# A fused residual add and layer norm on one Trainium2 core: turns of 8 rows instead of 4 on ScalarE and VectorE, and last stores of 8 and 8 rows instead of 12 and 4

## The chip, the cores and the metric

The kernel runs on one core of one Trainium2 chip. The metric is device time in microseconds (us) of one execution. Before the change it is 238.29 us (median of 3 runs, 238.26 to 238.30).

A "row" below is a set of 128 rows of the input, one for each partition: [128, 512] fp32, 256 KB. There are 128 such rows, numbered 0 to 127.

## The reference

```python
# x, residual: [16, 1024, 512] fp32; gamma = 1, beta = 0 in this draw; eps = 1e-5
def reference(x, residual, gamma, beta, eps):
    z = x + residual
    mean = np.mean(z, axis=-1, keepdims=True)
    var = np.var(z, axis=-1, keepdims=True)
    z_norm = (z - mean) / np.sqrt(var + eps)
    return (gamma * z_norm + beta).astype(np.float32)
```

x and residual are read (67 MB), the result is written (34 MB).

## The kernel before

SyncE (SP) issues all bulk transfers into one DMA queue, in the order of a written plan. `x48+16` loads rows 48 to 63 of x, `r` loads residual, `o` stores. The buffer of z holds 64 rows, that of residual 32, so a load of x waits for an old store to land, and a load of residual waits for POOL's adds.

```python
PLAN = """
x0+8 r0+8 x8+8 r8+8 x16+16 r16+16 x32+16 r32+16
x48+16 r48+16 o0+16 r64+16 x64+16 o16+16 r80+16 x80+16
o32+16 r96+16 x96+8 x104+8 o48+16 r112+16 x112+8 x120+8
o64+16 o80+16 o96+16 o112+12 o124+4
"""
ADDS = [4, 4, 8] * 7 + [4] * 4     # rows of one POOL add
TURN = 4                           # rows of one turn
SETS = 2                           # turns in one loop body
LAP = SETS * TURN
```

POOL adds residual into z. ScalarE takes a turn of rows: it makes their means (one pass for each row), then their sums of squares (a second pass), then one square-root for the whole turn. VectorE follows with two passes of its own and a reciprocal.

```python
    with act.Fori(0, total // LAP) as lap:            # ScalarE, a loop on the chip
        ...
        for j in range(SETS):                         # unrolled in the body
            due = act.snap(r0 + (j + 1) * TURN)
            act.wait_ge(s_dve, due)
            act.wait_ge(s_add, due)
            for k in range(TURN):
                i = act.activation(out=junk_m[k][:, :], in_=zk[k], func=ACT.Identity,
                                   scale=-inv_d, accum_out=nm[j][:, k : k + 1])
            i.then_inc(s_mean, TURN)
            act.wait_ge(s_mean, due)
            for k in range(TURN):
                i = act.activation(out=junk_s[k][:, :], in_=zk[k], func=ACT.Square,
                                   bias=nm[j][:, k : k + 1], accum_out=ssq[j][:, k : k + 1])
            i.then_inc(s_ssq, TURN)
            act.wait_ge(s_ssq, due)
            act.activation(out=std[j][:, :], in_=ssq[j][:, :], func=ACT.Sqrt, ...).then_inc(s_std, TURN)
    ...
    with dve.Fori(0, total // LAP) as lap:            # VectorE
        ...
        for j in range(SETS):
            dve.wait_ge(s_ssq, due)
            for k in range(TURN):                     # first pass: (z - mean) * gamma
                dve.scalar_tensor_tensor(out=zk[k], in0=zk[k], scalar=nm[j][:, k : k + 1], ...)
            dve.wait_ge(s_std, due)
            dve.reciprocal(out=rstd[j][:, :], in_=std[j][:, :]).then_inc(s_dve, TURN)
            dve.wait_ge(s_dve, due + LAP)
            for k in range(TURN):                     # second pass: * rstd + beta
                i = dve.scalar_tensor_tensor(out=zk[k], ..., scalar=rstd[j][:, k : k + 1], ...)
            i.then_inc(s_out, TURN)                   # stores wait for this
```

## Time and profile before

| | before |
|---|---|
| time | 238.29 us |
| span in the profile | 236.9 us |
| share of the span in which the bulk queue moves data | 99.2% |
| ScalarE, VectorE, POOL busy | 185.5, 177.2, 143.0 us |
| last add lot of POOL starts / last store issued | 192.86 (four adds) / 226.67 us |

From the profile page of the kernel before. Part 1 is busy time by engine; part 3 is the DMA queues with packets, MB and the share of 16 engines' span; part 5 gives, for each group of instructions, the count, busy us and mean ns, and then the idle time ahead of them and what ended it.

```profile
PE 3.7 (2%) x4; PEld 1.2 (0%) x4; DVE 177.2 (75%) x290; ACT 185.5 (78%) x545; POOL 143.0 (60%) x29
...
q1 hardware_dynamic: 4176, 100.67, 99.2%
q14 instruction: 1, 0.01, 0.0%
...
L202 ACT ACTIVATE junk_m<-zbuf 128x512 f32 x128 | 74.9, 585 | 29.1 <-POOL zbuf L180 27.5
L212 ACT ACTIVATE junk_s<-zbuf,nm 128x512 f32 x128 | 88.8, 694 | 1.0
...
L221 ACT ACTIVATE std<-ssq,eps_t 128x4 f32<-128x4 f32 x32 | 9.5, 297 | 3.0
L249 DVE RECIPROCAL rstd<-std 128x4 f32<-128x4 f32 x32 | 5.5, 170 | 0.0
```

No engine is near 100%; the queue q1 is. Queue q14, whose kind the page gives as instruction, has one packet in the whole span.

The table of windows of the kernel before: the stretch in us, then busy us of each engine, the granted clock, the DMA share and GB/s.

```profile
77.00:80.00 3.00, 0.00 (x0) 0.00 (x0) 2.71 (x5) 2.89 (x11) 1.80 (x1) 1.00 1.16 448
190.00:230.00 40.00, 0.00 (x0) 0.00 (x0) 30.39 (x49) 26.16 (x77) 17.96 (x4) 1.00 1.00 432
230.00:231.00 1.00, 0.00 (x0) 0.00 (x0) 0.00 (x0) 0.00 (x0) 0.00 (x0) 1.00 1.03 442
231.00:232.00 1.00, 0.00 (x0) 0.00 (x0) 0.00 (x0) 0.00 (x0) 0.00 (x0) 1.00 0.97 418
232.00:233.00 1.00, 0.00 (x0) 0.00 (x0) 0.00 (x0) 0.00 (x0) 0.00 (x0) 1.00 0.85 360
233.00:236.00 3.00, 0.00 (x0) 0.00 (x0) 0.00 (x0) 0.00 (x0) 0.00 (x0) 1.00 0.71 300
236.00:237.00 1.00, 0.00 (x0) 0.00 (x0) 0.00 (x0) 0.00 (x0) 0.00 (x0) 1.00 0.02 8
```

The queue runs at 432 GB/s from 190 to 230 us; the rate falls as the last store drains (360 GB/s at 232 to 233 us, 300 from there to 236).

The end of the kernel before in the timeline (start us, duration, engine, line, operation; SPq is SyncE issuing a transfer).

```profile
178.18 0.80 SPq L146 DMA_DIRECT2D zbuf<-in_x_dram  x2
...
192.86 17.96 POOL L180 TENSOR_TENSOR zbuf<-zbuf,rbuf 128x2048 f32<-128x2048 f32 x4 [11.62 <-DMA zbuf<-in_x_dram]
...
221.03 0.30 ACT L221 ACTIVATE std<-ssq,eps_t 128x4 f32<-128x4 f32 x1
...
223.92 2.72 DVE L252 SCALAR_TENSOR_TENSOR zbuf<-zbuf,rstd,beta_p 128x512 f32 x4
226.67 0.33 SPq L146 DMA_DIRECT2D out_dram<-zbuf  x1
```

SyncE issues the last loads of x at 178.18 us, because a store has landed. POOL starts its last four adds at 192.86, because the load of rows 112 to 119 has landed. VectorE's last four rows take from 223.92 to 226.64, and the last store (4 rows) is issued at once, while older stores still fill the queue for some six microseconds.

### The profile page before, as it was taken

Reading aid. Unit: us, or ns where it says so; the run is one execution under the profiler, and the core shown is the slowest. Engines: PE = TensorE matmul, PEld = TensorE weight load, DVE = VectorE, ACT = ScalarE, POOL = GpSimd, SP = SyncE. Lnnn points to the kernel's source line nnn. Section 1 sums busy time; section 2 is a strip of 40 time slices with the busy share of each in tenths; the row PEclk is TensorE's granted clock in tenths of the full one; section 3 lists DMA queues with packets and bytes.
Section 4 is the critical chain, followed back from the end, with each engine's and each line's share of the span. In section 5 each row is a group of like instructions: output and inputs, shape, how many; then the busy total and the mean of one; then the engine's idle time right before and its main releaser. Section 6 shows DMA issues by size and latency. Waiting matters only on the chain.

```text
span 236.9 us, 1471 instructions
## 1 busy us (share of the span) xinstructions
PE 3.7 (2%) x4; PEld 1.2 (0%) x4; DVE 177.2 (75%) x290; ACT 185.5 (78%) x545; POOL 143.0 (60%) x29
## 2 busy tenths in 40 slices
PE   0600000000000000000000000000000000000000
PEld 0100000000000000000000000000000000000000
DVE  0001977939699999999898989896989895698920
ACT  2019879497999999999999998979998956999300
POOL 0098920999799699604995059944995049950000
DMA  8999999999999999999999999999999999999996
GB/s 310 443 432 426 426 443 443 443 443 443 426 415 398 443 443 443 426 420 409 431 437 443 443 443 432 420 407 429 443 437 437 409 432 448 437 420 437 426 430 285
DMA packets 4181, 100.68 MB, mean 425 GB/s; under 512 B 466, under 2 KB 466, under 8 KB 468
## 3 DMA queue, kind: packets, MB, share of 16 engines
q1 hardware_dynamic: 4176, 100.67, 99.2%
q14 instruction: 1, 0.01, 0.0%
q10 hardware_dynamic: 4, 0.00, 0.0%
HBM read 67.11 MB, written 33.55 MB: 425 GB/s over the span
## 4 chain that ended last, share of the span: by engine, by line
DMA 71%; POOL 9%; ACT 9%; DVE 2%; issue 2%; SPq 1%; ACTq 0%; DVEq 0%; POOLq 0%
DMA out_dram<-zbuf 49%; DMA rbuf<-in_residual_dram 16%; POOL zbuf L180 9%; DMA zbuf<-in_x_dram 6%; ACT junk_s L212 5%; ACT junk_m L202 4%; SPq L146 1%; DVE zbuf L240 1%; DVE zbuf L252 1%; ACTq L202 0%; DVEq L240 0%; ACT std L221 0%; DVE rstd L249 0%; ACTq L193 0%; POOLq L177 0%
## 5 line engine op out<-in xcount | busy, mean ns | idle before, releaser
L180 POOL TENSOR_TENSOR zbuf<-zbuf,rbuf 128x2048 f32<-128x2048 f32 (+1 forms) x25 | 142.8, 5740 | 67.6 <-DMA zbuf<-in_x_dram 40.8
L240 DVE SCALAR_TENSOR_TENSOR zbuf<-zbuf,nm,gamma_p 128x512 f32 x128 | 87.1, 743 | 46.3 <-ACT junk_s L212 46.3
L202 ACT ACTIVATE junk_m<-zbuf 128x512 f32 x128 | 74.9, 585 | 29.1 <-POOL zbuf L180 27.5
L212 ACT ACTIVATE junk_s<-zbuf,nm 128x512 f32 x128 | 88.8, 694 | 1.0
L252 DVE SCALAR_TENSOR_TENSOR zbuf<-zbuf,rstd,beta_p 128x512 f32 x128 | 87.1, 743 | 1.1
L212 ACT ACTIVATION_READ_ACCUMULATOR junk_s<-zbuf,nm 128x1 f32 x128 | 23.9, 187 | 0.0
L202 ACT ACTIVATION_READ_ACCUMULATOR junk_m<-zbuf 128x1 f32 x128 | 23.9, 187 | 0.0
L221 ACT ACTIVATE std<-ssq,eps_t 128x4 f32<-128x4 f32 x32 | 9.5, 297 | 3.0
L249 DVE RECIPROCAL rstd<-std 128x4 f32<-128x4 f32 x32 | 5.5, 170 | 0.0
L190 ACT ACT_TABLE_LOAD x1 | 1.3, 1283 | 2.7 <-PEq L60 2.7
L132 PE MATMUL gamma_p<-gb_row,ones 1*128 1x512 f32 x2 | 2.0, 1119 | 7.2 <-DMA gb_row<-in_gamma_dram 7.2
L132 PE MATMUL beta_p<-gb_row,ones 1*128 1x512 f32 x2 | 1.9, 1052 | 0.0
L127 DVE MEMSET ones<- 1x128 f32 x1 | 0.2, 165 | 2.0 <-PEq L60 2.0
L132 PEld LDWEIGHTS beta_p<-gb_row,ones 1*128 1x128 f32 x2 | 0.7, 328 | 1.0 <-issue 0.5
L132 PEld LDWEIGHTS gamma_p<-gb_row,ones 1*128 1x128 f32 x2 | 0.5, 308 | 7.1 <-issue 7.1
L288 POOL MEMSET const-float32-0.0<- 128x1 f32 x1 | 0.1, 98 | 0.2 <-issue 0.2
L288 POOL MEMSET const-bfloat16-1.0<- 128x1 bf16 x1 | 0.1, 101 | 0.0
L288 POOL MEMSET const-uint8-127<- 128x1 uint8 x1 | 0.1, 101 | 0.0
L288 POOL MEMSET const-float32-1.0<- 128x1 f32 x1 | 0.1, 98 | 0.0
L128 DVE MEMSET eps_t<- 128x1 f32 x1 | 0.1, 59 | 0.0
## 6 DMA issues: line engine op xcount, KB each, us to landing
rbuf<-in_residual_dram SPq DMA_DIRECT2D x7, 4096.0 KB, 30.5
out_dram<-zbuf SPq DMA_DIRECT2D x7, 4096.0 KB, 28.6
zbuf<-in_x_dram SPq DMA_DIRECT2D x5, 4096.0 KB, 28.9
zbuf<-in_x_dram SPq DMA_DIRECT2D x6, 2048.0 KB, 14.9
rbuf<-in_residual_dram SPq DMA_DIRECT2D x2, 2048.0 KB, 15.7
out_dram<-zbuf SPq DMA_DIRECT2D x1, 3072.0 KB, 13.5
out_dram<-zbuf SPq DMA_DIRECT2D x1, 1024.0 KB, 10.2
gb_row<-in_gamma_dram ACTq DMA_DIRECT2D x1, 2.0 KB
```

The source lines that it names most:

```text
L127: nc.vector.memset(ones[:, :], 1.0).then_inc(s_const, 1)
L132: nc.tensor.matmul(dest[:, :], ones[:, :], gb_row[:, k * D : (k + 1) * D], start=True, stop=True).then_inc(s_pe, 1)
L146: i = nc.sync.dma_start(out=out, in_=in_).then_inc(s, 16)
L180: nc.gpsimd.tensor_tensor(out=z, in0=z, in1=part(rbuf, R_ROWS, lo, n), op=ALU.add).then_inc(s_add, n)
L190: act.preload_act_table_set("sqrt_and_others")
L202: i = act.activation(out=junk_m[k][:, :], in_=zk[k], func=ACT.Identity, scale=-inv_d, accum_out=nm[j][:, k : k + 1],)
L212: i = act.activation(out=junk_s[k][:, :], in_=zk[k], func=ACT.Square, bias=nm[j][:, k : k + 1], accum_out=ssq[j][:, k : k + 1],)
L221: act.activation(out=std[j][:, :], in_=ssq[j][:, :], func=ACT.Sqrt, bias=eps_t[:, 0:1], scale=inv_d,).then_inc(s_std, TURN)
L240: dve.scalar_tensor_tensor(out=zk[k], in0=zk[k], scalar=nm[j][:, k : k + 1], in1=gamma_p[:, :], op0=ALU.add, op1=ALU.mult,)
L249: dve.reciprocal(out=rstd[j][:, :], in_=std[j][:, :]).then_inc(s_dve, TURN)
L252: i = dve.scalar_tensor_tensor(out=zk[k], in0=zk[k], scalar=rstd[j][:, k : k + 1], in1=beta_p[:, :], op0=ALU.mult, op1=ALU.add,)
L288: nc = _bacc.Bacc("TRN2", target_bir_lowering=False, num_devices=1)
```

## The change

Its intent: fewer turns, so fewer square-roots, reciprocals and waits (half of each), with semaphore steps of 4 rows inside a turn so that a neighbour need not wait for the whole turn. The last two stores become 8 and 8 rows, since rows now become ready by turns of 8. Two turns stay unrolled in each loop body, so a body now handles 16 rows instead of 8. The scratch outputs of ScalarE's two passes become one set, six of eight in PSUM.

```diff
@@ -20,16 +20,16 @@
 x0+8 r0+8 x8+8 r8+8 x16+16 r16+16 x32+16 r32+16
 x48+16 r48+16 o0+16 r64+16 x64+16 o16+16 r80+16 x80+16
 o32+16 r96+16 x96+8 x104+8 o48+16 r112+16 x112+8 x120+8
-o64+16 o80+16 o96+16 o112+12 o124+4
+o64+16 o80+16 o96+16 o112+8 o120+8
 """
 
 
-TURN = 4
-SETS = 2
-LAP = SETS * TURN
+TURN = 8
+HALF = TURN // 2
+LAP = 2 * TURN
 ... (scratch tensors)
+    def turns(eng):
+        with eng.Fori(0, total // LAP) as lap:
+            z0 = eng.snap((lap * (LAP * D)) % (Z_ROWS * D))
+            r0 = eng.snap(lap * LAP)
+            for j in range(2):
+                due = eng.snap(r0 + (j + 1) * TURN)
+                zk = [zbuf[:, bass.ds(z0 + (j * TURN + i) * D, D)] for i in range(TURN)]
+                yield j, due, zk
 ... (ScalarE; the old loop removed)
+    for j, due, zk in turns(act):
+        act.wait_ge(s_dve, due)
+        for k in range(TURN):
+            if k % HALF == 0:
+                act.wait_ge(s_add, due - (HALF - k))
+            i = act.activation(out=junk[k][:, :], in_=zk[k], func=ACT.Identity, ...)
+        i.then_inc(s_mean, TURN)
+        act.wait_ge(s_mean, due)
+        for k in range(TURN):
+            i = act.activation(out=junk[k][:, :], in_=zk[k], func=ACT.Square, ...)
+            if k % HALF == HALF - 1:
+                i.then_inc(s_ssq, HALF)
+        act.wait_ge(s_ssq, due)
+        act.activation(out=std[j][:, 0:TURN], in_=ssq[j][:, 0:TURN], func=ACT.Sqrt, ...)
 ... (VectorE; the old loop removed)
+    for j, due, zk in turns(dve):
+        for k in range(TURN):
+            if k % HALF == 0:
+                dve.wait_ge(s_ssq, due - (HALF - k))
+            dve.scalar_tensor_tensor(out=zk[k], in0=zk[k], scalar=nm[j][:, k : k + 1], ...)
+        dve.wait_ge(s_std, due)
+        dve.reciprocal(out=rstd[j][:, 0:TURN], in_=std[j][:, 0:TURN]).then_inc(s_dve, TURN)
+        dve.wait_ge(s_dve, due + LAP)
+        for k in range(TURN):
+            i = dve.scalar_tensor_tensor(out=zk[k], ..., scalar=rstd[j][:, k : k + 1], ...)
+            if k % HALF == HALF - 1:
+                i.then_inc(s_out, HALF)
```

More of the change, by code (lines that the diff above doesn't have):

```diff
@@ L84 @@
     nm, ssq, std, rstd = (
-        [nc.alloc_sbuf_tensor(f"{name}{j}", [P, TURN], FP32) for j in range(SETS)]
+        [nc.alloc_sbuf_tensor(f"{name}{j}", [P, TURN], FP32) for j in range(2)]
         for name in ("nm", "ssq", "std", "rstd")
@@ L89 @@
     beta_p = nc.alloc_psum_tensor("beta_p", [P, D], FP32)
-    junk_m = [nc.alloc_psum_tensor(f"junk_m{i}", [P, D], FP32) for i in range(TURN)]
-    junk_s = [nc.alloc_psum_tensor(f"junk_s{i}", [P, D], FP32) for i in range(6 - TURN)]
-    junk_s += [
-        nc.alloc_sbuf_tensor(f"junk_s{i}", [P, D], FP32) for i in range(6 - TURN, TURN)
-    ]
+    junk = [nc.alloc_psum_tensor(f"junk{i}", [P, D], FP32) for i in range(6)]
+    junk += [nc.alloc_sbuf_tensor(f"junk{i}", [P, D], FP32) for i in range(6, TURN)]
     sems = []
@@ L192 @@
     act.sem_inc(s_dve, LAP)
-    with act.Fori(0, total // LAP) as lap:
-        z0 = act.snap((lap * (LAP * D)) % (Z_ROWS * D))
-        r0 = act.snap(lap * LAP)
-        for j in range(SETS):
-            due = act.snap(r0 + (j + 1) * TURN)
-            act.wait_ge(s_dve, due)
-            act.wait_ge(s_add, due)
-            zk = [zbuf[:, bass.ds(z0 + (j * TURN + k) * D, D)] for k in range(TURN)]
-            for k in range(TURN):
-                i = act.activation(
-                    out=junk_m[k][:, :],
-                    in_=zk[k],
-                    func=ACT.Identity,
-                    scale=-inv_d,
-                    accum_out=nm[j][:, k : k + 1],
-                )
-            i.then_inc(s_mean, TURN)
-            act.wait_ge(s_mean, due)
-            for k in range(TURN):
-                i = act.activation(
-                    out=junk_s[k][:, :],
-                    in_=zk[k],
-                    func=ACT.Square,
-                    bias=nm[j][:, k : k + 1],
-                    accum_out=ssq[j][:, k : k + 1],
-                )
-            i.then_inc(s_ssq, TURN)
-            act.wait_ge(s_ssq, due)
-            act.activation(
-                out=std[j][:, :],
-                in_=ssq[j][:, :],
-                func=ACT.Sqrt,
-                bias=eps_t[:, 0:1],
-                scale=inv_d,
-            ).then_inc(s_std, TURN)
@@ new lines @@
+    for j, due, zk in turns(act):
[3 more added lines that the diff above has]
+                act.wait_ge(s_add, due - (HALF - k))
+            i = act.activation(
+                out=junk[k][:, :],
+                in_=zk[k],
+                func=ACT.Identity,
+                scale=-inv_d,
+                accum_out=nm[j][:, k : k + 1],
+            )
+        i.then_inc(s_mean, TURN)
+        act.wait_ge(s_mean, due)
+        for k in range(TURN):
+            i = act.activation(
+                out=junk[k][:, :],
+                in_=zk[k],
+                func=ACT.Square,
+                bias=nm[j][:, k : k + 1],
+                accum_out=ssq[j][:, k : k + 1],
+            )
+            if k % HALF == HALF - 1:
+                i.then_inc(s_ssq, HALF)
+        act.wait_ge(s_ssq, due)
+        act.activation(
+            out=std[j][:, 0:TURN],
+            in_=ssq[j][:, 0:TURN],
+            func=ACT.Sqrt,
+            bias=eps_t[:, 0:1],
+            scale=inv_d,
+        ).then_inc(s_std, TURN)
@@ L230 @@
     dve = nc.vector
     dve.wait_ge(s_pe, 2)
-    with dve.Fori(0, total // LAP) as lap:
-        z0 = dve.snap((lap * (LAP * D)) % (Z_ROWS * D))
-        r0 = dve.snap(lap * LAP)
-        for j in range(SETS):
-            due = dve.snap(r0 + (j + 1) * TURN)
-            zk = [zbuf[:, bass.ds(z0 + (j * TURN + k) * D, D)] for k in range(TURN)]
-            dve.wait_ge(s_ssq, due)
-            for k in range(TURN):
-                dve.scalar_tensor_tensor(
-                    out=zk[k],
-                    in0=zk[k],
-                    scalar=nm[j][:, k : k + 1],
-                    in1=gamma_p[:, :],
-                    op0=ALU.add,
-                    op1=ALU.mult,
-                )
-            dve.wait_ge(s_std, due)
-            dve.reciprocal(out=rstd[j][:, :], in_=std[j][:, :]).then_inc(s_dve, TURN)
-            dve.wait_ge(s_dve, due + LAP)
-            for k in range(TURN):
-                i = dve.scalar_tensor_tensor(
-                    out=zk[k],
-                    in0=zk[k],
-                    scalar=rstd[j][:, k : k + 1],
-                    in1=beta_p[:, :],
-                    op0=ALU.mult,
-                    op1=ALU.add,
-                )
-            i.then_inc(s_out, TURN)
@@ new lines @@
+    for j, due, zk in turns(dve):
+        for k in range(TURN):
+            if k % HALF == 0:
+                dve.wait_ge(s_ssq, due - (HALF - k))
+            dve.scalar_tensor_tensor(
+                out=zk[k],
+                in0=zk[k],
+                scalar=nm[j][:, k : k + 1],
+                in1=gamma_p[:, :],
+                op0=ALU.add,
+                op1=ALU.mult,
+            )
+        dve.wait_ge(s_std, due)
+        dve.reciprocal(out=rstd[j][:, 0:TURN], in_=std[j][:, 0:TURN]).then_inc(s_dve, TURN)
+        dve.wait_ge(s_dve, due + LAP)
+        for k in range(TURN):
+            i = dve.scalar_tensor_tensor(
+                out=zk[k],
+                in0=zk[k],
+                scalar=rstd[j][:, k : k + 1],
+                in1=beta_p[:, :],
+                op0=ALU.mult,
+                op1=ALU.add,
+            )
+            if k % HALF == HALF - 1:
+                i.then_inc(s_out, HALF)
```

## The prediction

> **What bounds the kernel now.** The DMA queue. The page's queue part gives it 99.2% busy for 100.67 MB; the table of windows gives a DMA share of 1.00 and 430 to 432 GB/s from 10 to 230 us (1.16 at 77 to 80 us, where loads turn to stores). [...] 432 to 434 in most microseconds. ScalarE (78% busy) and VectorE (75%) only have to stay ahead of the stores. In the SP's waits, mid-kernel issues wait for POOL's adds and landed stores, which the change doesn't move; VectorE is waited for three times (46 us) at the last stores, while older transfers still fill the queue.
>
> **What the change does.** A ScalarE turn of 4 rows costs 5.85 us (timeline at 203 us: four means 2.59, four squares 2.94, square-root and restart 0.32). A turn of 8 I work out as 5.03 + 5.76 + 0.32 = 11.1 us instead of 11.7: some 9 us saved over the kernel. Square-roots (297 ns) and reciprocals (170 ns) go from 32 to 16 each. Row work is unchanged. All this is off the critical path for 200 us.
>
> On the path is the tail. The last add lots end at 197.4, 201.8, 206.3, 210.8 us. After, rows 112 to 119 need eight means before any square, so they wait for the lot at 201.8:
> - turn A: squares 204.6 to 210.4; VectorE's second pass 213.4 to 218.8, first of the last two stores issued near 219 (before: 12 rows at 220.9);
> - turn B: means 210.7 to 215.8, squares to 221.5 (before 220.9). VectorE then has four first passes, a reciprocal and eight second passes left (8.5 us) instead of four and four (5.7), ending near 230.0, against 226.64.
>
> So the last store is issued 3.3 us later and is twice as big (2 MB). Does the queue run dry? In the packets of the trace the engines finish the 12-row store at 232.4 to 233.1 us, one laggard at 233.9. Four rows fewer (1 MB, 2.42 us at 433 GB/s) gives 230.0 to 230.7, laggard 231.5. At the kernel's start the first packet follows its issue by 1.01 us [...]. So packets restart near 231.1: a gap of 0.4 to 1.1 us on most engines, none on the laggard, which ended the kernel (236.41, the others by 235.6). Add 4.9 us for 2 MB: end 236.0 to 236.4. The gap is mostly hidden behind the laggard.
>
> **Prediction.** 238.4 us (before 238.29), range 238.0 to 239.5. Chances: faster by over 2% 0.01, within 2% 0.97, slower 0.02.
>
> **Signs it is right.** ScalarE busy down about 5 us, VectorE about 2.5; ScalarE's wait for POOL up. Last VectorE pass ends at 229.5 to 230.5. A short dip of the DMA rate near 231 us, nowhere else. Issues up to 179 us within 0.3 us of before. The last store's issue to landing falls from 10.2 to about 6.9 us.
>
> **What would make it wrong.** Fresh packets starting over 1.3 us after the issue, or VectorE ending later than 230.5 (each 0.1 us then shows at the end); ScalarE paying more for squares; the laggard changing (a gain of up to 0.4 us). A late mid-kernel store would make issues before 179 us slip; their slack, about 10 us, says no.

## The result, and the profile after

The changed kernel takes 239.75 us (median of 6 runs, 239.28 to 240.35) against 238.30 for the kernel before in the same rounds (6 runs, 238.21 to 238.54): ratio 1.006, 95% interval 1.0045 to 1.0074. Slower by 0.6% is "the same" at 2%, but it is clear of the noise, and it lies outside the range that was predicted (238.0 to 239.5).

The profile page of the changed kernel, the same lines.

```profile
PE 3.7 (2%) x4; PEld 1.2 (0%) x4; DVE 174.8 (73%) x274; ACT 178.8 (75%) x529; POOL 143.0 (60%) x29
...
q1 hardware_dynamic: 4176, 100.67, 98.8%
q14 instruction: 2, 0.02, 0.0%
...
L203 ACT ACTIVATE junk<-zbuf 128x512 f32 x128 | 75.7, 592 | 40.1 <-POOL zbuf L176 38.6
L213 ACT ACTIVATE junk<-zbuf,nm 128x512 f32 x128 | 87.3, 683 | 0.5
...
L223 ACT ACTIVATE std<-ssq,eps_t 128x8 f32<-128x8 f32 x16 | 4.8, 301 | 1.5
L247 DVE RECIPROCAL rstd<-std 128x8 f32<-128x8 f32 x16 | 3.1, 196 | 0.0
```

The engines did get cheaper, as intended: ScalarE is busy 6.7 us less, VectorE 2.4 us less. The queue is busy for a smaller share of a longer span. And q14 carried two packets instead of one.

The table of windows of the changed kernel.

```profile
77.00:80.00 3.00, 0.00 (x0) 0.00 (x0) 2.50 (x5) 3.00 (x11) 2.69 (x1) 1.00 1.06 371
190.00:230.00 40.00, 0.00 (x0) 0.00 (x0) 32.49 (x52) 26.77 (x80) 17.93 (x4) 1.00 1.00 432
230.00:231.00 1.00, 0.00 (x0) 0.00 (x0) 1.00 (x3) 0.00 (x0) 0.00 (x0) 1.00 0.27 115
231.00:232.00 1.00, 0.00 (x0) 0.00 (x0) 0.63 (x1) 0.00 (x0) 0.00 (x0) 1.00 0.15 66
232.00:233.00 1.00, 0.00 (x0) 0.00 (x0) 0.00 (x0) 0.00 (x0) 0.00 (x0) 1.00 0.66 279
233.00:236.00 3.00, 0.00 (x0) 0.00 (x0) 0.00 (x0) 0.00 (x0) 0.00 (x0) 1.00 1.02 431
236.00:237.00 1.00, 0.00 (x0) 0.00 (x0) 0.00 (x0) 0.00 (x0) 0.00 (x0) 1.00 1.23 524
```

The gap near 231 us was predicted, but it is much deeper: two microseconds nearly empty while VectorE is still at work (1.00 and 0.63 us busy in them). The lines at 77 to 80 us, where loads turn to stores, must be read with care: a window counts each packet whole where it starts (hence the share of 1.16), so the 448 and 371 GB/s depend on the edges. Over 70 to 90 us the windows give 424 before and 418 after: a small loss, which was not predicted.

The end of the changed kernel in the timeline.

```profile
179.97 0.80 SPq L142 DMA_DIRECT2D zbuf<-in_x_dram  x2
...
194.66 17.93 POOL L176 TENSOR_TENSOR zbuf<-zbuf,rbuf 128x2048 f32<-128x2048 f32 x4 [11.29 <-DMA zbuf<-in_x_dram]
...
223.36 0.30 ACT L223 ACTIVATE std<-ssq,eps_t 128x8 f32<-128x8 f32 x1
...
226.28 5.36 DVE L250 SCALAR_TENSOR_TENSOR zbuf<-zbuf,rstd,beta_p 128x512 f32 x8
231.66 0.33 SPq L142 DMA_DIRECT2D out_dram<-zbuf  x1
```

Here is the surprise. The issue of the last loads, at 178.18 us before, is at 179.97, and POOL starts its last adds at 194.66 instead of 192.86: 1.8 us late, before the tail has begun. From there on the tail runs just as predicted (last add start to last VectorE end: predicted 37.1 us, measured 37.0). So the question is not the tail but what made the loads land late. The issue at 178.18 us waits for the store of rows 48 to 63 (o48). The median engine ends that store at 177.03 us before and at 177.16 after, but the last engine at 177.65 before and at 179.55 after (from the packets, see below): the store is late on single engines, not as a whole.

### Which DMA engine lands last

The trace of the kernel before has 464 packets of 4 bytes in the bulk queue for 29 transfers, so 16 for each. They are taken here as one from each of the 16 DMA engines (the profile counts shares of 16), written when its share of the transfer is done. The issue that waits for o48 comes 0.53 us after the last of that store's 16 (0.42 in the changed kernel), so the slowest engine decides when a transfer has landed. So for every transfer one can compute how far the slowest engine is behind the median engine. Call it the lag. The next table (worked out from the packets of each run's trace, not a view of the profile) has the lag after five loads and two stores, all runs together; rows of x48 land near 70 us, o0 near 90, x64 near 109, x80 near 138, x104 near 167, x120 near 196, o96 near 225. "Instruction packets" are the starts of the 8 KB packets of the instruction queue within the run. "Last data packet" is when the last data packet ends.

```
run          instruction   lag of the slowest engine after      last store  last data  median
             packets, us   x48  o0   x64  x80  x104 x120 o96    issued us   packet us  of runs
before       225.4         0.19 0.24 0.24 0.20 0.35 0.62 0.98   226.67      236.41     238.29
t4_88        226.0         0.20 0.31 0.34 0.37 0.66 0.84 1.28   226.82      236.59     238.38
b_seed_late  226.1         0.23 0.27 0.22 0.24 0.44 0.67 1.03   226.57      236.34     238.42
b_sp24_late  225.5         0.33 0.20 0.20 0.21 0.39 0.65 1.07   226.66      236.40     238.25
t8_short     34.5          0.47 0.42 0.42 0.45 0.42 0.62 1.10   230.59      236.49     238.39
changed      35.8, 46.9    1.04 1.41 1.89 2.41 2.38 2.44 2.44   231.66      237.84     239.75
after_again  35.9, 46.7    0.90 1.38 1.94 2.55 2.49 2.43 2.42   231.58      237.69     239.55
t8_124       35.8, 46.9    0.93 1.61 2.67 2.72 2.92 3.06 3.05   231.78      239.97     241.59
a_pad70      10.5, 10.9    0.91 1.28 1.79 2.04 2.02 1.96 1.96   231.03      237.09     239.44
t4_lap16     35.9, 46.7    0.79 1.18 1.42 2.25 2.21 2.16 2.16   227.84      237.34     239.32
b_padA       21.3          0.59 0.68 0.84 1.35 1.98 2.14 2.13   227.82      237.29     238.95
b_pad        22.3, 27.3    0.84 1.32 1.96 2.15 2.13 2.48 2.48   228.07      237.64     239.48
b_pad70      10.2, 11.0    0.89 1.48 2.22 2.31 2.50 2.74 2.74   228.19      237.79     239.16
b_seed       34.6          0.59 0.62 2.01 2.85 2.84 2.79 2.79   228.93      238.00     238.68
b_sp24       227.2         0.96 1.70 2.27 2.40 2.40 2.80 2.79   228.20      237.91     239.55
```

The first and the sixth line are the two kernels. In the kernel before the slowest engine stays within 0.24 us of the median for 140 us. In the changed kernel two engines fall back early, and the worse of them reaches 2.4 us by 138 us. The packets show when: one 32 KB packet next to an instruction packet takes 1.59 us at 36.1 us, another 1.88 us at 47.2, where 1.21 us is the median. Then, as far as the packets can be put together by engine (they do not name it), the same two engines lose more in a handful of places: near 78 to 79, 108, 137 to 139 and 167 us, which are the times at which the queue goes from a load to a store (r48 to o0, x64 to o16, x80 to o32, x104 to o48). Not each of the two loses at each turn: the worse one loses at the first three, the other little until 137 us. Near 108, 137 and 167 us the late engine is still in its last load packets when the others begin to store, and these packets take 1.4 to 1.7 us (the one of half the size near 167 us 1.12 instead of 0.61). Near 78 us the last load packets of nearly all engines are slow (1.5 to 1.8 us; the kernel before has eleven packets of 1.45 to 1.68 there too), and one of the worst engine takes 2.2.

### The profile page after: what moved, and what is told of

Read it like the earlier page. It is cut to its first block, busy times and chain, and to the rows that moved or that the text cites. A ratio compares the mean times of both kernels' runs of the same rounds, so it can differ in the third digit from the quotient of the medians.

```text
span 238.2 us, 1327 instructions
## 1 busy us (share of the span) xinstructions
PE 3.7 (2%) x4; PEld 1.2 (0%) x4; DVE 174.8 (73%) x274; ACT 178.8 (75%) x529; POOL 143.0 (60%) x29
## 3 DMA queue, kind: packets, MB, share of 16 engines
q1 hardware_dynamic: 4176, 100.67, 98.8%
## 4 chain that ended last, share of the span: by engine, by line
DMA 46%; ACT 18%; DVE 14%; POOL 11%; issue 5%; SPq 1%; DVEq 1%; ACTq 1%; POOLq 0%
DMA out_dram<-zbuf 24%; DMA rbuf<-in_residual_dram 16%; POOL zbuf L176 11%; ACT junk L213 10%; ACT junk L203 8%; DVE zbuf L238 7%; DVE zbuf L250 7%; DMA zbuf<-in_x_dram 6%; SPq L142 1%; DVEq L238 1%; ACTq L203 1%; DVE rstd L247 0%; ACTq L186 0%; DVEq L186 0%; DVEq L248 0%
## 5 line engine op out<-in xcount | busy, mean ns | idle before, releaser
L203 ACT ACTIVATE junk<-zbuf 128x512 f32 x128 | 75.7, 592 | 40.1 <-POOL zbuf L176 38.6
L213 ACT ACTIVATE junk<-zbuf,nm 128x512 f32 x128 | 87.3, 683 | 0.5
L250 DVE SCALAR_TENSOR_TENSOR zbuf<-zbuf,rstd,beta_p 128x512 f32 x128 | 85.7, 743 | 0.6
L203 ACT ACTIVATION_READ_ACCUMULATOR junk<-zbuf 128x1 f32 x128 | 23.9, 187 | 0.0
L213 ACT ACTIVATION_READ_ACCUMULATOR junk<-zbuf,nm 128x1 f32 x128 | 23.9, 187 | 0.0
L223 ACT ACTIVATE std<-ssq,eps_t 128x8 f32<-128x8 f32 x16 | 4.8, 301 | 1.5
L247 DVE RECIPROCAL rstd<-std 128x8 f32<-128x8 f32 x16 | 3.1, 196 | 0.0
```

The costliest lines, as they stand in the source:

```text
L203: i = act.activation(out=junk[k][:, :], in_=zk[k], func=ACT.Identity, scale=-inv_d, accum_out=nm[j][:, k : k + 1],)
L213: i = act.activation(out=junk[k][:, :], in_=zk[k], func=ACT.Square, bias=nm[j][:, k : k + 1], accum_out=ssq[j][:, k : k + 1],)
L223: act.activation(out=std[j][:, 0:TURN], in_=ssq[j][:, 0:TURN], func=ACT.Sqrt, bias=eps_t[:, 0:1], scale=inv_d,).then_inc(s_std, TURN)
L247: dve.reciprocal(out=rstd[j][:, 0:TURN], in_=std[j][:, 0:TURN]).then_inc(s_dve, TURN)
L250: i = dve.scalar_tensor_tensor(out=zk[k], in0=zk[k], scalar=rstd[j][:, k : k + 1], in1=beta_p[:, :], op0=ALU.mult, op1=ALU.add,)
```

## The experiments

Thirteen kernels were run; each was correct. Each was timed in five runs (t8_124 in four), the first of them profiled. The kernel before ran beside each set on the same chip: 238.30, 238.11, 238.25 and 238.20 us in the four sets.

Two theories stood at first:

- **F**: the longer loop bodies (about 90 records per lap on ScalarE instead of 50, 60 instead of 34 on VectorE, counted in the traces) bring instruction traffic to the DMA engines (the packets of 8 KB at 35.8 and 46.9 us), which sets single engines back.
- **L**, the rival: the last store simply comes too late, and how far an engine lags is chance.

### after_again: the changed kernel once more

No edit.

> The changed kernel again, for a second trace and more times. Both theories expect 239.3 to 240.3 us. Theory F (the longer loop bodies of ScalarE and VectorE cost the queue something: one or two DMA engines fall behind the others during the run, so loads land late, the last adds start late and the last store is issued near 231.5 instead of 230.0): the slowest engine again finishes the first of the two last stores 1.8 us or more after the median engine (2.44 us in the first trace, 1.0 us in the kernel before), in a second trace too. Rival L (the last store simply comes too late; how far an engine lags is chance): the lag in this second trace is anything between 0.3 and 2.5 us, and the time follows the end of the last VectorE pass.

Measured: 239.55 us (239.30 to 239.74), ratio 1.0052 (1.0039 to 1.0066); instruction packets at 35.9 and 46.7 us again, the slowest engine 2.4 us behind at the end again, last store issued at 231.58. The lag is not chance: two traces of the changed kernel show the same packets at the same times and the same growth.

### t4_lap16: the long loop body alone

```diff
-SETS = 2
+SETS = 4
```

(on the kernel before: turns of 4 rows and all stores as before, but four turns in one body.)

> The kernel before with four turns of 4 rows in a loop body instead of two (16 rows a lap, as in the changed kernel), its stores and steps as before. Theory F: the slowest DMA engine lags the median by 1.8 us or more at the end, and the time is 239.0 to 240.0. Rival L: nothing of what it blames is here, so 238.2 to 238.5 us and a lag of about 1.0 us as before.

Measured: 239.32 us (239.08 to 239.64), ratio 1.0048 (1.0034 to 1.0062). Instruction packets at 35.9 and 46.7 us, as in the changed kernel; lag 2.16 us. This kernel has none of the other parts of the change. Unrolling the loop body twice as far costs 1.0 us by itself. Its last store is issued at 227.84, early enough; what ends it is the engine that lags.

### t4_88: the store sizes alone

```diff
-o64+16 o80+16 o96+16 o112+12 o124+4
+o64+16 o80+16 o96+16 o112+8 o120+8
```

> The kernel before with last stores of 8 and 8 rows instead of 12 and 4. Rows are ready at 226.6 us, before the queue runs dry near 230, so both theories expect 238.2 to 238.6 us. If it is 239 or more, the store sizes themselves cost (theory S).

Measured: 238.38 us (238.09 to 238.47), ratio 0.9999 (0.9985 to 1.0013). With turns of 4, the split of the last stores is free.

### t8_124: the changed kernel with the old split

The same edit the other way round, on the changed kernel.

> The changed kernel with the last stores of 12 and 4 rows as before. The queue now runs dry near 232.5 instead of 230. Rival L: with the last rows ready near 230 to 231.6 the gap is gone or halved, 238.2 to 238.6 us. Theory F: the engine that lags by about 2.4 us ends the kernel near 237.8 in the trace, so 239.0 to 239.9 us, though no gap is left on the other engines.

Measured: 241.59 us (241.32 to 241.93), ratio 1.0137. Both expectations missed, and the fault was mine: a store of 12 rows up to row 123 needs the first half of the last turn's second pass, so it was issued only at 229.15, while most engines had ended the store before it by 225.3. Most of the 16 engines stood empty for 4.7 us (packets start 0.82 to 0.97 us after this issue); the late ones had a packet now and then until 228.4. So with turns of 8 the split of 8 and 8 is worth 2.0 us against after_again; that part of the change is sound. The run says nothing between F and L.

### b_pad, b_padA, b_pad70, a_pad70: shifting the loops in the instruction stream

To see whether the length of the body matters or where it lies, useless semaphore increments were put ahead of the loops of otherwise unchanged kernels: in the kernel before 30 on ScalarE and 45 on VectorE (b_pad), 30 on ScalarE alone (b_padA), 70 on both (b_pad70); in the changed kernel 70 on both (a_pad70).

```diff
     act.sem_inc(s_dve, LAP)
+    for _ in range(30):
+        act.sem_inc(s_pad[0], 1)
 ...
+    for _ in range(45):
+        dve.sem_inc(s_pad[1], 1)
     dve.wait_ge(s_pe, 2)
```

> The kernel before, with 30 (ScalarE) and 45 (VectorE) semaphore increments of no use ahead of the two loops; the loops themselves are as before. Theory F1 (what costs is where the loop lies in the instruction stream[...]): [...] Instruction packets then stand in the trace in the first laps, near 20 to 45 us, two DMA engines lag by 1.5 us or more, and the time is 239.0 to 240.5 (twice the laps, so perhaps more than 1 us). Rival F2 (the length of the loop body, whatever its place): 238.2 to 238.6 us and a lag of about 1 us.

> The same for ScalarE alone (30 increments). F1: one DMA engine lags by 1.5 us or more instead of two, one instruction packet early in the trace; 239.0 to 240.5 us. F2: as before, 238.2 to 238.6.

> The kernel before with 70 increments ahead of each loop[...]. A control for the cost of the increments themselves. Both theories: no lag beyond 1.0 us, 238.1 to 238.5 us.

> The changed kernel with the same 70 increments ahead of each loop. F1: [...] the lag of the slowest engine falls from 2.4 to about 1 us or less, the last loads land near 193, the last store is issued near 230.0, and the time is 238.2 to 238.9 us, what the prediction said. F2 and L: 239.3 to 240.0 us as without them.

Measured, with the kernel before at 238.11 us beside them:

| run | time (range) | ratio (95%) | instruction packets |
|---|---|---|---|
| b_pad | 239.48 (239.34 to 239.69) | 1.0059 (1.0046 to 1.0073) | 22.3, 27.3 us |
| b_padA | 238.95 (238.72 to 239.20) | 1.0032 (1.0019 to 1.0046) | 21.3 us |
| b_pad70 | 239.16 (239.11 to 239.68) | 1.0048 (1.0034 to 1.0061) | 10.2, 11.0 us |
| a_pad70 | 239.44 (238.82 to 239.61) | 1.0053 (1.0039 to 1.0067) | 10.5, 10.9 us |

The loops of the kernel before, unchanged but moved, cost up to what the changed kernel costs: one packet early in the run comes with one slow engine and 0.84 us (b_padA, just under the 239.0 us that was expected), two with 1.37 us (b_pad) and 1.05 us (b_pad70). So a loop body of the old length brings the packets too when it lies elsewhere in the stream. The controls with 70 increments missed: they were meant to put the loops at a place that brings no instruction packet (an estimate of mine; such a place was not shown), but packets came at 10 to 11 us, with loads already under way. As controls for the increments themselves they therefore failed: the runs with increments alone do not separate their cost from that of the packets. t4_lap16 above and b_sp24 below, which have no increments, do. The runs correct the theory: it is not a cost per lap (b_pad has 16 laps and two packets). One packet (b_padA) or two, between 10 and 47 us, were enough in these kernels. The lag grows afterwards without further packets, mostly at the turns from loads to stores, whether a lap has 8 rows (b_pad, 0.84 us after x48 and 2.15 after x80) or 16 (the changed kernel, 1.04 and 2.41). Call this theory **G**.

### t8_short: the changed kernel with a short loop body

One turn of 8 rows in a body, the two sets of statistics picked by a register. Turns, semaphore steps and stores are those of the changed kernel.

```diff
-        with eng.Fori(0, total // LAP) as lap:
+        with eng.Fori(0, total // TURN) as lap:
 ...
+            p0 = eng.snap((lap * TURN) % (2 * TURN))
 ...
-                accum_out=nm[j][:, k : k + 1],
+                accum_out=nm[:, bass.ds(p0 + k, 1)],
 (and so on for ssq, std, rstd)
```

> The changed kernel with one turn of 8 rows in a loop body (its two sets of statistics picked by a register instead of by unrolling), so the loop bodies are about as short as before; turns, steps and stores are those of the changed kernel. What the runs so far say (theory G): an instruction packet of 8 KB in the first part of the run puts one DMA engine some 0.6 us behind, and that engine falls further behind each time the queue goes from loads to stores (near 79, 108, 137, 167, 196 us). Theory G: no instruction packet before 200 us, the slowest engine about 1.0 to 1.3 us behind the median at the end of the store before last, last store issued 229.8 to 230.4, time 238.2 to 238.9 us. Rival L (the late last store itself): 239.3 to 240.0.

Measured: 238.39 us (238.24 to 238.87), ratio 1.0012 (0.9999 to 1.0026): the time that was predicted for the changed kernel. The part of the expectation about instruction packets missed: one came, at 34.5 us, apparently on an engine that was ahead of the others, for no engine got more than 0.47 us behind by 70 us, and the lag did not grow before 177 us. So in this run a packet that left no engine clearly behind the others did no harm. The last store was issued 0.2 us later than expected. From the timeline of t8_short:

```profile
178.08 0.80 SPq L142 DMA_DIRECT2D zbuf<-in_x_dram  x2
...
192.77 17.95 POOL L176 TENSOR_TENSOR zbuf<-zbuf,rbuf 128x2048 f32<-128x2048 f32 x4 [11.54 <-DMA zbuf<-in_x_dram]
...
225.21 5.36 DVE L249 SCALAR_TENSOR_TENSOR zbuf<-zbuf,rstd,beta_p 128x512 f32 x8
230.59 0.33 SPq L142 DMA_DIRECT2D out_dram<-zbuf  x1
```

And from its table of windows:

```profile
230.00:231.00 1.00, 0.00 (x0) 0.00 (x0) 0.57 (x1) 0.00 (x0) 0.00 (x0) 1.00 0.20 82
231.00:232.00 1.00, 0.00 (x0) 0.00 (x0) 0.00 (x0) 0.00 (x0) 0.00 (x0) 1.00 0.62 262
232.00:233.00 1.00, 0.00 (x0) 0.00 (x0) 0.00 (x0) 0.00 (x0) 0.00 (x0) 1.00 1.26 524
233.00:236.00 3.00, 0.00 (x0) 0.00 (x0) 0.00 (x0) 0.00 (x0) 0.00 (x0) 1.00 1.03 437
```

The loads are issued and land when they did before; the last store is still 3.9 us later than before, there is still a gap near 231 us, and yet it costs next to nothing, since one engine was 1.1 us behind in the last stores in any case. Rival L falls as the cause: a last store 3.9 us late and its gap were there without the loss. (A store later still, as in the changed kernel, does cost; see below.)

### b_seed and b_seed_late: an ordinary load in place of the instruction packet

On the kernel before, two useless loads of 6 and 4 KB, meant to delay one DMA engine (b_seed has 8 packets in q10 instead of 4: one of data and one of 4 bytes for each load), issued by ScalarE ahead of its loop (executed near 21 us), or after its loop (225 us).

```diff
+    act.wait_ge(s_pe, 2)
+    act.wait_ge(s_add, 4)
+    for t, n, s in ((seed_t, 3, s_seed[0]), (gb_row, 2, s_seed[1])):
+        act.dma_start(
+            out=t[:, :], in_=xf[0:n, :].rearrange("a d -> (a d)")[None, :]
+        ).then_inc(s, 16)
```

> The kernel before with two small loads of no use, of 6 and 4 KB, [...] at about 17 us, issued by ScalarE before its loop. No other change. Theory G (any delay of one engine early in the run grows at each turn from loads to stores): the engine that carries them is 0.4 to 0.8 us behind by 31 us and 1.6 us or more at the end; 238.6 to 239.4 us. Rival H (it is the instruction packets and what goes with them lap by lap, not a delay as such): the engine stays 0.3 to 0.6 us behind, no more, and the time is 238.0 to 238.4.

> The same two small loads at about 221 us, after ScalarE's loop, when no turn from loads to stores is left. Both theories: nothing grows, at most 0.4 us at the end if they fall on the engine that ends last: 238.1 to 238.6 us.

Measured: b_seed 238.68 us, but scattered (239.74 in the profiled run, the others 238.09 to 238.68), ratio 1.0011 (0.9998 to 1.0025); b_seed_late 238.42 (238.20 to 238.69), ratio 1.0009 (0.9995 to 1.0023). The trace of b_seed shows two slow engines at the end, 2.8 and 1.8 us behind, but with the added instructions ahead of ScalarE's loop an instruction packet came too, at 34.6 us. One of its larger losses (0.62 us, at 91.5 us) came soon after a turn from stores to loads, so not every loss falls on a turn from loads to stores. The run is inconclusive between a delay as such and something that comes with the packets.

### b_sp24 and b_sp24_late: a delay of one engine, by itself

So the delay was put into the main queue, by SyncE, which leaves the instruction streams of ScalarE and VectorE alone: a useless copy of 24 KB in device memory that runs on one engine (4178 packets in q1 instead of 4176: one of data and one of 4 bytes), ahead of x32 in the queue, or ahead of o80. On the kernel before.

```diff
+    spare = nc.dram_tensor("spare", [1, 12 * D - 1], FP32).ap()
 ...
     for kind, lo, n in moves:
+        if (kind, lo) == ("x", 32):       # b_sp24_late: ("o", 80)
+            nc.sync.dma_start(
+                out=spare, in_=xf[0:12, :].rearrange("a d -> (a d)")[None, : 12 * D - 1]
+            ).then_inc(s_seed, 16)
```

> The kernel before with one copy of no use of 24 KB from device memory to device memory on one DMA engine, in the main queue ahead of the load of rows 32 to 47, so at about 41 us. Theory G (a delay of one engine as such grows at each turn from loads to stores): that engine is 0.8 to 1.5 us behind by 50 us and 2 us or more at the end of the run, 0.8 us or more beyond its first delay; no instruction packet before 200 us; 238.8 to 239.9 us. Rival H (only instruction packets do it): the engine stays as far behind as it was at 50 us, and the time is 238.1 to 238.7.

> The same copy ahead of the store of rows 80 to 95, so at about 206 us, after the last turn from loads to stores. Both theories: the engine ends 0.8 to 1.5 us behind, no growth, 238.1 to 238.8 us. G says that b_sp24 is at least 0.5 us slower than this one, H says that they are equal.

Measured: b_sp24 239.55 us (239.44 to 239.62), ratio 1.0055 (1.0042 to 1.0069); b_sp24_late 238.25 (238.18 to 238.44), ratio 1.0003 (0.9989 to 1.0017). The copy takes 0.91 us of one engine in both, at 40.8 and at 206.3 us. Early it costs 1.35 us, late nothing. In the trace of b_sp24 no instruction packet comes before 227 us, and the one engine loses 0.91 us at 40.8, then 0.59 at 78.1, 0.52 at 79.9, 0.58 at 108.3, 0.19 at 137.9 and 0.47 at 196.2 us beyond the usual time of its packets, most of it at the turns from loads to stores. In b_sp24_late the delayed engine happened not to be the one that ends last, and hides behind it (the last data packet of the run ends at 236.40 us, in the kernel before at 236.41).

The end of the run in the windows of b_sp24:

```profile
230.00:233.00 3.00, 0.00 (x0) 0.00 (x0) 0.00 (x0) 0.00 (x0) 0.00 (x0) 1.00 0.93 399
233.00:236.00 3.00, 0.00 (x0) 0.00 (x0) 0.00 (x0) 0.00 (x0) 0.00 (x0) 1.00 0.70 295
236.00:237.00 1.00, 0.00 (x0) 0.00 (x0) 0.00 (x0) 0.00 (x0) 0.00 (x0) 1.00 0.08 33
237.00:238.00 1.00, 0.00 (x0) 0.00 (x0) 0.00 (x0) 0.00 (x0) 0.00 (x0) 1.00 0.04 16
```

No gap here: the queue fades out, and from 236 us one engine or two work alone (a full engine is a share of 0.0625). G holds, and the rival H, that only instruction packets do it, falls.

## Why the prediction was right or wrong

- **What bounds the kernel.** Right: the DMA queue, before and after (99.2% and 98.8%).
- **What the change removes.** Right in kind: VectorE fell by 2.4 us (2.5 predicted), ScalarE by 6.7 (5 predicted; the square-roots gave 4.7 of it, the squares 1.5, going from 694 to 683 ns with six of eight scratch outputs in PSUM, and the means cost 0.8 more; the rest is not in these lines, and that the scratch outputs made the squares faster was not tested by itself). None of it was on the path: ScalarE's wait for POOL rose from 27.5 to 38.6 us.
- **The tail.** Right: from the start of the last adds to the end of VectorE 37.0 us against 37.1 predicted. First packets follow the last issue by 0.83 to 0.98 us on most engines (1.01 predicted). In t8_short, where nothing else is in the way, the gap hides behind the engine that ends last, as predicted, and the time is 238.39 us (238.4 predicted). That it fits so closely is partly luck: its last store was issued at 230.59, 0.6 us later than predicted, and its first packets came 0.03 to 0.17 us sooner after the issue.
- **The step that failed:** "mid-kernel issues wait for POOL's adds and landed stores, which the change doesn't move", with its sign "Issues up to 179 us within 0.3 us of before". The issue at 178.18 us moved to 179.97. The prediction counted work on the compute engines and took the lags of the 16 DMA engines from the trace of before as given. The runs showed in its place: the longer loop bodies bring two instruction packets at 36 and 47 us (none before 225 us in the kernel before); each sets one DMA engine back (the packets next to them take 1.59 and 1.88 us instead of 1.21); and an engine that is back loses more at most of the turns from loads to stores, until it is 2.4 us behind instead of 1.0. The store of rows 48 to 63 then lands on its last engine at 179.55 us instead of 177.65, and the last loads, which wait for it, come 1.8 us late. The prediction had named "a late mid-kernel store" and dismissed it because of a slack of "about 10 us". But the store was not late as a whole (its median engine ended 0.13 us later than before); it was late on its slowest engine, which a slack in the issues does not cover.
- **How that becomes 1.45 us.** The engine that lags would by itself end the kernel late: 1.0 us in t4_lap16, which has no gap at all. It also delays the last adds and so the last store, from about 230 to 231.66 us, which empties the other engines for two microseconds, so that they end late too (237.5 us, the slowest at 237.84). The two parts are not to be added: they overlap. Against t8_short, which has the same tail, the last store is issued 1.07 us later, the median engine ends 1.1 us later (237.5 against 236.4) and the slowest 1.35: so in the changed kernel most of the cost came by way of the late loads and the late last store.
- **What stays open.** Why the place of a loop in the instruction stream decides whether instruction packets come in the run is not shown. Why a late engine loses time when the others turn to stores is not shown; the runs show that it does, when and how much. Nor is there a firm threshold: lags of 0.59 us and more at 70 us grew in every trace, while in the other traces, with 0.47 and less, none passed 0.66 by 167 us, but in b_seed an engine that was 0.40 us behind at 70 us was among those that were 0.6 us behind by 80 us and grew from there. No kernel was run with the turns from loads to stores taken away. And the 1.0 us by which one engine ends late in the kernel before, which builds up after 140 us (0.35 by 148 us), was not looked into.

No version beat the kernel before. The best one with turns of 8, t8_short, equals it, as it should where the queue is the limit.

## What to carry to other kernels

When the DMA queue is the limit, look at its 16 engines one by one, not at its mean: a transfer lands with its slowest engine (o48 of the changed kernel at 179.55 us, its median engine at 177.16), and a small delay of one engine early in a run can outlast and outgrow its cause (0.91 us at 40.8 us became a lag of 2.8 us by 196 us in b_sp24). A change that only unrolls a loop further (t4_lap16: packets at 35.9 and 46.7 us), or adds instructions ahead of it (b_padA: at 21.3 us), can bring an instruction packet into the busy part of the run; check the instruction queue's packets and their times before and after. A short loop body is no guarantee: b_pad has the short body of the kernel before and cost 1.37 us. The saving here was on engines off the critical path and was worth nothing, so a small side effect on the path decided the sign.
